# A list scheduler given measured durations and new ranks, and the last output tile cut in the middle

## The chip, the cores and the metric

The kernel runs on one core of a Trainium2 chip, in one launch. The metric is the device time of that launch in microseconds, as the median of several runs. TensorE (PE) multiplies matrices, VectorE (DVE) and ScalarE (ACT) work on tiles in SBUF and PSUM, GpSimd (POOL) on tiles in SBUF alone, and SyncE (SP) issues the transfers.

## The reference

One transformer block on 512 tokens of width 1024, in float32. In short:

```python
h = rmsnorm(x, attn_pre_g)
q_n, kc, vc, ksl, vsl, kwn, vwn, g_n, q_s, k_s, v_s = split(h @ w_in)
# 8 heads: compressed + selected + windowed attention, gated; 8 heads: 128-wide window with sinks
o_nsa = gate0 * attend(q_n, compress(kc), compress(vc)) + gate1 * attend(q_n, ksl, vsl) + gate2 * attend(q_n, kwn, vwn)
o_swa = window_attend(q_s, k_s, v_s, sinks)
x = x + rmsnorm(concat(o_nsa, o_swa) @ w_o, attn_post_g)
a, u = split(rmsnorm(x, mlp_pre_g) @ w_gate_up)            # 2 x 2816
y = (gelu(causal_conv3(a)) * u) @ w_down
x = x + rmsnorm(y, mlp_post_g)
out = x + (p @ w_ple) * sigmoid(x @ w_ple_gate)
```

## The kernel before, in words

Every large product is made of three matmuls on values split in a high part and a low part (`hi*hi + lo*hi + hi*lo`). So each operand, weights, probabilities and activations alike, costs a rounding copy (the high part, on ScalarE) and a subtraction (the low part, on VectorE or GpSimd) before TensorE can use it.

The stages: loading and the value projections; compression of keys and values; the first query projections; then the *planned part*: attention, the other projections, the output projection, its norm, the per-layer embedding and the first products of the MLP; then the MLP with its own written order, and the last gate.

The planned part is emitted by class `Plan`. Each operation is added with a name (a tuple), an engine, a duration in us, a rank, the operations it comes after, and the buffers that it takes and uses. `Plan.order` is a list scheduler: it keeps a clock for each engine and again and again picks the operation that can start first by the given durations; among those that are ready when their engine is free, the lowest rank goes first. The operations are emitted in that order and each engine executes its own in that order. The durations thus never reach the chip, only the order does.

Attention is cut in 16 units, `ORDER`: a kind (nsa or swa), a group of 4 heads and a tile of 128 queries. A unit's ranks are its number less one for scores and softmax, its number for the products. Operations are known by their first letter(s) and the length of the name, which is how `SHIFT` re-ranks a kind:

- `s`: scores on TensorE into one of three banks `ps` (L598, L599). `m`: on VectorE the biased minimum of such a bank, called a *soft* here (L602; 4 fields for nsa, 3 for swa), which frees the bank. `e`: the exponential on ScalarE (L606). `rc`: reciprocals on VectorE (L714, L724). `px`, `pe`, `pr`: the same for the compressed branch, on POOL, ScalarE and VectorE. `gc`, `pm`: the gate column of the compressed branch and its multiplication, on POOL. `g`: scaling of a head's probabilities on POOL (L594).
- `t`: transposes of the probabilities on TensorE into one of two banks `pt` (L807, for the compressed block L800). `h` and `l`: high part on ScalarE (L811) and low part on VectorE (L815) of such a bank, for the compressed block in four pieces of 32 rows (`l` with 4 fields, L834). The last of them frees the bank. `v`: the products with the values (L822, L839). `up`, `ad`, `oh`, `ol`: the sum of the two halves of the result, and its high and low parts.
- `f`: steps of the projections (L258 to L262) and `op`: steps of the output projection (L1001 to L1003), three matmuls each. They rank behind everything of the units and are called *fill*: TensorE takes them when nothing of the units can start. Their weights need `w` (a load on SP), `wh` (ScalarE) and `wl` (POOL, L915); the output projection's need `ow`, `oh` (3 fields) and `ol`. `hi` are high parts of later weights.

The last stage, `ple_gate`, makes 8 output tiles. The last one is cut in two runs of columns, so that its end is short:

```python
pieces = [(0, T)] if c < KC - 1 else [(0, LASTCUT), (LASTCUT, T)]
for n, (a, b) in enumerate(pieces):
    ...
    self.gemm(ps[:, a:b], wt, [x[:, :, a:b] for x in self.x2])
    ...
    nc.scalar.activation(s, ps[:, a:b], AF.Sigmoid)
    nc.vector.tensor_mul(s, s, self.e[c // 2][:, c % 2, a:b])
    ...
    nc.sync.dma_start(io["out"][c * P : (c + 1) * P, a:b], o)
```

Of the kernel before, what the change touches and what calls it, by code (L numbers as in the profile page):

```python
# [49 lines left out]
YTAG = ["kn"] * 3 + ["tt"] + ["p"] * 2 + ["pt"] * 2 + ["u"] * 14  # L50


LASTCUT = 352
FORMS = (-5.6, 5.5)
NPLAIN = 5
SEVEN = range(8, NFF)
# [13 lines left out]
PAIRS = 2  # L70
THIRD = (NCMP + 2 * T) // 3
UNITS = 3
SHIFT = {("l", 4): 0.88, ("pe2", 2): -4.0, ("v", 4): 1.95, ("oe", 3): -1.52, ("e", 3): 1.52, ("s", 4): -0.33,
         ("pm", 2): 1.91, ("pn", 2): -0.47, ("g", 4): 1.14, ("oh", 2): 0.97, ("fe", 3): 0.12, ("rc", 3): -1.18,
         ("gc", 2): 1.04, ("m", 4): 0.11, ("n", 4): -2.1}
ORDER = [(k, g, qt) for k in "ns" for g in range(2) for qt in (3, 0, 2, 1)]
PLE_PS = ["mm", "s", "mm", "s", "mm", "s", "o", "s"]
ETAG = ["pt", "u", "u", "u"]
# [4 lines left out]
class Plan:  # L83
# [15 lines left out]

    def add(self, name, eng, us, rank, f, after=(), take=(), use=(), land=0.0, beside=None):  # L100
        assert name not in self.ops, name
        if rank < 100:
            rank += SHIFT.get((name[0], len(name)), 0.0)
        self.ops[name] = (eng, us, rank, f, [a for a in after if a], list(take), land, beside)
        for _, token in take:
            self.users.setdefault(token, set()).add(name)
        for token in use:
            self.users.setdefault(token, set()).add(name)
# [74 lines left out]
class Block:  # L183
# [1244 lines left out]
    def up_rest(self, pending):  # L1428
# [37 lines left out]
        def sums(j, n):  # L1466
            m0, m1 = w[j]["m"]
            if n == 0:
                w[j]["s13"] = self.u([P, D], F32, "pt")
                keep(add(w[j]["s13"][:, :W], m1[:, :W], m1[:, W:]))  # L1470
            s13 = w[j]["s13"]
            if n == 1:
                w[j]["s24"] = self.u([P, D], F32, "tt")
                keep(sub(w[j]["s24"][:, :W], s13[:, :W], m0[:, :W]))
            if n == 2:
                keep(sub(w[j]["s24"][:, W:], m0[:, W:], w[j]["s24"][:, :W]))  # L1476
            if n == 3:
                keep(sub(s13[:, W:], m0[:, :W], m1[:, :W]))
# [29 lines left out]
        def evict(j, n):  # L1508
            z = st[j]
            a = self.am[j % 2]  # L1510
            if n == 0:
                z["s"] = self.sp.tile([P, H], F32, tag="s1", name=self.nm("s1"), bufs=2)
                keep(act.activation(z["s"], z["p"][0], AF.Copy))
                z["e"] = self.s([P, 2, H], tag="as")
            if n in (1, 3):
                keep(act.activation(z["e"][:, n // 2, :], z["p"][0], AF.Copy))
            if n == 2:
                keep(add(a[:, 2 : 2 + H], z["s"], z["p"][1]))
            if n == 4:
                keep(add(z["e"][:, 1, :], z["e"][:, 1, :], z["p"][2]))  # L1520
            if n == 6:
                keep(add(a[:, 2 + H :], z["e"][:, 0, :], z["p"][2]))  # L1522
# [434 lines left out]
    def ple_gate(self):  # L1957
# [3 lines left out]
        for c in range(KC):  # L1961
            if c < NB:
                ps = self.pss[c]
            else:
                wt = ahead.get(c) or self.weight(io["wpg"][c])
            pieces = [(0, T)] if c < KC - 1 else [(0, LASTCUT), (LASTCUT, T)]
            for n, (a, b) in enumerate(pieces):
# [85 lines left out]
```

## Time and profile before

| | |
|---|---|
| median of 3 runs | 643.38 us (643.23 to 643.42) |
| the profiled execution's own time | 642.44 us |
| its span, first to last instruction | 640.7 us |
| TensorE busy | 633.0 us |
| VectorE, ScalarE, GpSimd busy | 532.1, 385.3, 128.1 us |
| planned attention in the trace | about 80 to 205 us |
| granted TensorE clock, mean | 0.999 |

A row of the timeline has the start and the duration in us, the engine, the line, the operation, out<-in by the program's names without their numbers, the shape and a count. An idle time of the engine before it stands in brackets with what ended it. Consecutive matmuls overlap in their records: the next starts before the record of the last has ended. A row of stretches has, for each engine, the busy time and the number of instructions.

### The profile page before, as it was taken

To read this page: it belongs to the slowest core of one execution; us is meant where nothing else is said; L and a number is where in the kernel's file an instruction comes from. 1 tells how busy PE (TensorE), PEld (TensorE's weight loads), DVE (VectorE), ACT (ScalarE), POOL (GpSimd) and SP (SyncE) were. 2 spreads that over 40 slices of the span, in tenths; PEclk is the share of its full clock that TensorE was granted. 3 is DMA by queue.
4 is the path that set the end of the run, shared out by engine and by line. 5 is a ranking of instruction groups with operands and counts; after the bars stand their busy time and mean duration, and the time that the engine had idled before them with its cause. 6 is when DMAs were issued, how large, how long until landed. Compare 5 with 4: busy or idle time off the path is not lost.

```text
span 640.7 us, 10962 instructions
## 1 busy us (share of the span) xinstructions
PE 633.0 (99%) x3925; PEld 567.6 (89%) x3925; DVE 532.1 (83%) x1133; ACT 385.3 (60%) x746; POOL 128.1 (20%) x213
## 2 busy tenths in 40 slices
PE   8999999999999999999999999999999999999997
PEld 8988888788887888888889999999998899999986
DVE  7794778989897559799999999999978887796972
ACT  7453689889999456265565656556656444362351
POOL 1120398667585320111000000000000000000000
PEclk9999999999999999999999999999999999999999
DMA  8437632210216456322223324233222233485031
GB/s 306 144 125 236 166 94 75 58 50 27 74 61 220 153 196 252 123 69 97 99 100 132 110 89 132 71 128 127 63 68 65 80 103 120 120 321 221 1 132 67
DMA packets 27864, 78.07 MB, mean 122 GB/s; under 512 B 3489, under 2 KB 5025, under 8 KB 27809
## 3 DMA queue, kind: packets, MB, share of 16 engines
q1 hardware_dynamic: 27664, 77.28, 36.2%
q8 instruction: 31, 0.51, 0.3%
q14 instruction: 25, 0.20, 0.1%
q10 hardware_dynamic: 144, 0.08, 0.1%
HBM read 63.72 MB, written 6.29 MB: 109 GB/s over the span
## 4 chain that ended last, share of the span: by engine, by line
PE 91%; DVE 4%; ACT 3%; issue 1%; DMA 1%; ACTq 0%; DVEq 0%
PE strassen_pss L1505 3%; PE strassen_pss L1502 3%; PE strassen_pss L1506 3%; PE nsa_pst L807 2%; PE nsa_pso L822 2%; PE strassen_psmm L1502 2%; PE strassen_psmm L1505 2%; PE strassen_psmm L1506 2%; PE strassen_pst L1502 2%; PE strassen_pst L1505 2%; PE strassen_pst L1506 2%; PE r_pss L1189 2%; PE r_psmm L1189 2%; PE nsa_pss L598 1%; PE fill_psmm L261 1%; PE fill_psmm L262 1%
## 5 line engine op out<-in xcount | busy, mean ns | idle before, releaser
L594 POOL TENSOR_SCALAR nsa_u<-nsa_u,nsa_nrc,gate 128x512 f32<-128x512 f32 (+3 forms) x64 | 38.7, 617 | 43.5 <-PE nsa_pss L599 30.1
L1828 POOL TENSOR_TENSOR mlpdown_s<-mlpdown_s,mlpdown_s 128x512 f32<-128x512 f32 x1 | 1.3, 1297 | 197.3 <-ACT mlpdown_s L1826 197.3
L1464 DVE TENSOR_TENSOR strassen_u<-strassen_u,strassen_u 128x1024 fp32r<-128x1024 f32 x31 | 37.7, 1218 | 0.2 <-ACT strassen_u L1460 0.2
L606 ACT ACTIVATE nsa_u<-nsa_u,nsa_nnm 128x512 f32<-128x512 f32 (+3 forms) x64 | 35.3, 553 | 3.1 <-DVE nsa_nnm L602 2.8
L815 DVE TENSOR_TENSOR nsa_u<-nsa_pst,nsa_u 128x512 fp32r<-128x512 f32 x40 | 27.0, 688 | 9.8 <-ACT nsa_u L811 9.6
L1460 ACT ACTIVATE strassen_u<-strassen_u 128x1024 fp32r<-128x1024 f32 x31 | 32.4, 1049 | 0.4 <-DVE strassen_u L1476 0.4
L1538 DVE SCALAR_TENSOR_TENSOR strassen_s<-mlpup_u,cols,strassen_s 128x512 f32<-128x512 f32 x36 | 26.9, 748 | 1.5 <-ACT strassen_s L1536 0.9
L822 PE MATMUL nsa_pso<-nsa_u,vnatural_u 128*128 128x512 f32 x80 | 28.0, 422 | 0.0
L811 ACT ACTIVATE nsa_u<-nsa_pst 128x512 fp32r<-128x512 f32 x40 | 23.3, 594 | 4.7 <-PE nsa_pst L807 4.0
L602 DVE CUSTOM_DVE_ANT_0 nsa_u<-nsa_pss,biastables_u 128x320 f32<-128x320 f32 (+3 forms) x64 | 24.7, 413 | 1.0 <-PE nsa_pss L599 0.9
L807 PEld LDWEIGHTS nsa_pst<-ident,nsa_u 128*128 128x128 f32 x160 | 18.9, 140 | 6.9 <-issue 1.3
L1738 ACT ACTIVATE mlpdown_u<-mlpdown_u 128x1024 fp32r<-128x1024 f32 (+1 forms) x15 | 15.1, 1011 | 15.6 <-DVE mlpdown_u L1757 15.3
L807 PE MATMUL nsa_pst<-ident,nsa_u 128*128 128x128 f32 x160 | 23.5, 274 | 0.7 <-DVE nsa_u L815 0.5
L1742 DVE TENSOR_TENSOR mlpdown_u<-mlpdown_wr,mlpdown_u 128x640 fp32r<-128x640 f32 (+1 forms) x19 | 17.5, 919 | 7.0 <-ACT mlpdown_u L1738 4.1
L1738 ACT ACTIVATE mlpdown_u<-mlpdown_wr 128x640 fp32r<-128x640 f32 (+1 forms) x19 | 15.0, 788 | 13.8 <-DMA mlpdown_wr<-in_dn_dram 3.1
L1505 PE MATMUL strassen_pss<-strassen_u,strassen_u 128*128 128x256 f32 x80 | 22.5, 282 | 0.0
L1502 PE MATMUL strassen_pss<-strassen_u,strassen_u 128*128 128x256 f32 x80 | 22.5, 281 | 0.0
L1742 DVE TENSOR_TENSOR mlpdown_u<-mlpdown_u,mlpdown_u 128x1024 fp32r<-128x1024 f32 (+1 forms) x15 | 17.5, 1170 | 5.9 <-ACT mlpdown_u L1738 5.7
L1506 PE MATMUL strassen_pss<-strassen_u,strassen_u 128*128 128x256 f32 x80 | 22.4, 280 | 0.0
L1541 ACT ACTIVATE strassen_s<-strassen_s 128x512 f32<-128x512 f32 x18 | 11.4, 632 | 17.1 <-DVE strassen_s L1538 17.1
L1536 ACT ACTIVATE strassen_s<-mlpup_u,cols 128x512 f32<-128x512 f32 x18 | 14.7, 815 | 10.5 <-DVE mlpup_u L1522 10.4
L1464 DVE TENSOR_TENSOR strassen_u<-strassen_wr,strassen_u 128x1024 fp32r<-128x1024 f32 x17 | 20.7, 1218 | 0.3 <-ACT strassen_u L1460 0.3
(690 smaller groups left out, 2582.7 us busy)
## 6 DMA issues: line engine op xcount, KB each, us to landing
strassen_wr<-in_gu_dram SPq DMA_DIRECT2D x17, 512.0 KB, 4.2
strassen_u<-in_gu_dram SPq DMA_DIRECT2D x17, 512.0 KB, 3.3
mlpdown_wr<-in_dn_dram SPq DMA_DIRECT2D x9, 512.0 KB, 3.5
mlpdown_wr<-in_dnx_dram SPq DMA_DIRECT2D x10, 320.0 KB, 2.9
r_wr<-in_gu_dram SPq DMA_DIRECT2D x6, 512.0 KB, 3.2
projq_wr<-in_win_dram SPq DMA_DIRECT2D x5, 512.0 KB, 3.3
loadx_u<-in_xT_dram SPq DMA_DIRECT2D x8, 256.0 KB, 4.7
compress_u<-projk_u SPq DMA_DIRECT2D x16, 128.0 KB, 2.3
```

The costliest lines, as they stand in the source:

```text
L594: self.tc.keep_in_program_order(self.nc.gpsimd.tensor_scalar(ap, ap, col, gate, op0=ALU.mult, op1=ALU.mult))
L606: self.tc.keep_in_program_order(self.nc.scalar.activation(p, p, AF.Exp, bias=nm, scale=-1.0, accum_out=sm))
L807: keep(nc.tensor.transpose(pt[:, r * P : (r + 1) * P], src, self.ident))
L815: keep(nc.vector.tensor_sub(t[:, 1, :], u["pt", j], t[:, 0, :].bitcast(F32)))
L822: keep(nc.tensor.matmul(u["po"], v, u["t", j][:, part, :], start=start, stop=u["left"] == 0))
L1460: keep(act.activation(hi, src, AF.Copy))
L1464: keep(sub(lo, src, hi.bitcast(F32)))
L1502: r = mm(ps, hi[:, o], x[:, 0, :], start=fresh and p == 0, stop=False, skip_group_check=not fresh)
L1505: mm(ps, lo[:, o], x[:, 0, :], start=False, stop=False, skip_group_check=not fresh)
L1506: mm(ps, hi[:, o], x[:, 1, :], start=False, stop=p == Q - 1, skip_group_check=not fresh)
L1738: keep(act.activation(z[key, 0], z[key][:, :n], AF.Copy))
L1742: keep(eng.tensor_sub(z[key, 1], z[key][:, :n], z[key, 0].bitcast(F32)))
```

## The change

Three edits. `SHIFT` gets four new values and six new kinds: swa exps 0.3 sooner, the gated compressed probabilities (`pm`) 0.9 sooner, their gate column (`gc`) 1.1 later, nsa softs (`m`, 4 fields) 0.3 later; newly low parts of projection weights (`wl`) 1.3 sooner, low parts of probabilities (`l`, 3 fields) 1.2 sooner, high parts of output-projection weights 1.3 later, swa softs (`m`, 3 fields) 1.1 later, high parts of later weights 0.3 later, transposes 0.6 later. A table `TAKES` replaces durations in the planner, by kind, name length and the old value; TensorE's, but for transposes, are also raised by 1%. `LASTCUT` goes from 352 to 256.

```diff
-LASTCUT = 352
+LASTCUT = 256
 ...
-         ("pm", 2): 1.91, ("pn", 2): -0.47, ("g", 4): 1.14, ("oh", 2): 0.97, ("fe", 3): 0.12, ("rc", 3): -1.18,
-         ("gc", 2): 1.04, ("m", 4): 0.11, ("n", 4): -2.1}
+         ("pm", 2): 1.01, ("pn", 2): -0.47, ("g", 4): 1.14, ("oh", 2): 0.97, ("fe", 3): 0.12, ("rc", 3): -1.18,
+         ("gc", 2): 2.14, ("m", 4): 0.41, ("n", 4): -2.1, ("wl", 2): -1.3, ("l", 3): -1.2, ("oh", 3): 1.3,
+         ("m", 3): 1.1, ("hi", 2): 0.3, ("t", 3): 0.6}
 ...
+         ("pe", 2, 0.2): 0.201, ("oh", 2, 0.31): 0.308, ("oe", 3, 0.48): 0.494, ("l", 4, 0.21): 0.3,
+         ("rc", 3, 0.08): 0.178, ("rc", 3, 0.14): 0.26, ("pr", 2, 0.2): 0.38, ("ad", 3, 0.42): 0.431,
 ...
     def add(self, name, eng, us, rank, f, after=(), take=(), use=(), land=0.0, beside=None):
         assert name not in self.ops, name
+        us = TAKES.get((name[0], len(name), round(us, 2)), us)
+        if eng == "PE" and (name[0], len(name)) != ("t", 3):
+            us *= 1.01
         if rank < 100:
             rank += SHIFT.get((name[0], len(name)), 0.0)
```

From the tables on, lines of the changed kernel are numbered 10 higher. Three places show what the new order does. On TensorE, at the end of the last nsa unit and the start of the swa units (171 us in the trace of before): `nsa_pso` are products, `swa_pst` transposes, `swa_pss` scores, `fill_psmm` a step of the output projection. Before:

```order
L822 MATMUL nsa_pso_2256<-nsa_u_2276,vnatural_u_334 128x512
L807 MATMUL swa_pst_2306<-ident,swa_u_2135 128x128 x4
L822 MATMUL nsa_pso_2256<-nsa_u_2276,vnatural_u_334 128x512
L598 MATMUL swa_pss_2297<-projq_u_812,nsa_u_1791 128x256
L599 MATMUL swa_pss_2297<-projq_u_813,nsa_u_1791 128x256
L807 MATMUL swa_pst_2320<-ident,swa_u_2135 128x128 x4
L839 MATMUL nsa_pso_2256<-compressout_u_725,vc 128x256 x2
```

and now:

```order
L832 MATMUL nsa_pso_2253<-nsa_u_2268,vnatural_u_334 128x512 x2
L608 MATMUL swa_pss_2289<-projq_u_812,fill_u_1782 128x256
L609 MATMUL swa_pss_2289<-projq_u_813,fill_u_1782 128x256
L1011 MATMUL fill_psmm_2304<-nsa_u_1301,nsa_u_2112 128x512
L1012 MATMUL fill_psmm_2304<-nsa_u_1302,nsa_u_2112 128x512
L1013 MATMUL fill_psmm_2304<-nsa_u_1301,nsa_u_2113 128x512
L817 MATMUL swa_pst_2312<-ident,swa_u_2136 128x128 x4
L817 MATMUL swa_pst_2321<-ident,swa_u_2136 128x128 x4
L849 MATMUL nsa_pso_2253<-compressout_u_725,vc 128x256 x2
```

Both groups of transposes moved behind the scores and behind a step of fill; the two products, of the high and of the low part, stand together.

On VectorE, where units 0 to 3 meet (97 us in the trace of before): `compressout_u` are the four low pieces of unit 0's compressed block, `nsa_pss` the score banks that softs read. Before:

```order
L815 TENSOR_TENSOR nsa_u_1192<-nsa_pst_1176,nsa_u_1192 128x512
L834 TENSOR_TENSOR compressout_u_725<-nsa_pst_1169,compressout_u_725 32x128 x2
L714 RECIPROCAL nsa_nrc_985<-nsa_nsm_984 128x2
L834 TENSOR_TENSOR compressout_u_725<-nsa_pst_1169,compressout_u_725 32x128 x2
L602 ISA nsa_pc_986,nsa_nnm_983<-nsa_pss_1195,biastables_u_457 128x32
L602 ISA nsa_nnm_983 128x1
L602 ISA nsa_u_1194,nsa_nnm_983<-nsa_pss_1195,biastables_u_457 128x384
```

and now:

```order
L844 TENSOR_TENSOR compressout_u_725<-nsa_pst_1167,compressout_u_725 32x128 x4
L825 TENSOR_TENSOR nsa_u_1192<-nsa_pst_1174,nsa_u_1192 128x512
L612 ISA nsa_pc_979,nsa_nnm_976<-nsa_pss_1159,biastables_u_457 128x32
L612 ISA nsa_nnm_976 128x1
L612 ISA nsa_u_1158,nsa_nnm_976<-nsa_pss_1159,biastables_u_457 128x384
L612 ISA nsa_nnm_976 128x1
L724 RECIPROCAL nsa_nrc_978<-nsa_nsm_977 128x2
```

The low pieces stand together, with the reciprocal no longer between them, and they and the low part of unit 1 have moved ahead of one more head's softs (bank 1159; in the old order that head's softs came before all of these rows).

On GpSimd, at the second weight of the fill (85 us in the trace of before): `128x1024` is a weight's low part (`wl`), the `128x128` scalings are those of unit 1. Before:

```order
L737 TENSOR_TENSOR nsa_gc_1036<-nsa_nrc_828,gate 128x4
L594 TENSOR_SCALAR nsa_u_941<-nsa_u_941,nsa_nrc_939,gate 128x128 x6
L936 TENSOR_TENSOR fill_u_1065<-fill_s_973,fill_u_1065 128x512
L915 TENSOR_TENSOR nsa_u_1071<-fill_wr_846,nsa_u_1070 128x1024
L594 TENSOR_SCALAR nsa_u_941<-nsa_u_941,nsa_nrc_939,gate 128x128 x2
```

and now:

```order
L925 TENSOR_TENSOR fill_u_1000<-fill_wr_846,fill_u_999 128x1024
L727 TENSOR_TENSOR nsa_pc_942<-nsa_pc_942,nsa_nnm_939 128x128
L604 TENSOR_SCALAR nsa_u_910<-nsa_u_910,nsa_nrc_828,gate 128x512
L604 TENSOR_SCALAR nsa_u_943<-nsa_u_943,nsa_nrc_941,gate 128x128
L946 TENSOR_TENSOR fill_u_1064<-fill_s_1002,fill_u_1064 128x512
L604 TENSOR_SCALAR nsa_u_943<-nsa_u_943,nsa_nrc_941,gate 128x128 x7
```

The weight's low part stands ahead of all eight scalings of unit 1, where it stood behind six of them, and the gate column has moved further back.

More of the change, by code (lines that the diff above doesn't have):

```diff
@@ L72 @@
 UNITS = 3
-SHIFT = {("l", 4): 0.88, ("pe2", 2): -4.0, ("v", 4): 1.95, ("oe", 3): -1.52, ("e", 3): 1.52, ("s", 4): -0.33,
-         ("pm", 2): 1.91, ("pn", 2): -0.47, ("g", 4): 1.14, ("oh", 2): 0.97, ("fe", 3): 0.12, ("rc", 3): -1.18,
-         ("gc", 2): 1.04, ("m", 4): 0.11, ("n", 4): -2.1}
+SHIFT = {("l", 4): 0.88, ("pe2", 2): -4.0, ("v", 4): 1.95, ("oe", 3): -1.52, ("e", 3): 1.22, ("s", 4): -0.33,
[3 rows of a table added]
+TAKES = {("h", 3, 0.47): 0.496, ("h", 4, 0.26): 0.282, ("up", 2, 0.5): 0.51, ("nh", 2, 0.53): 0.62,
[5 rows of a table added]
 ORDER = [(k, g, qt) for k in "ns" for g in range(2) for qt in (3, 0, 2, 1)]
```

3 rows, old and new, of the table TAKES are left out of this document.

## The prediction

> **What bounds the kernel now.** I read the page's first part, then the busy time of each engine in stretches, then TensorE's waits, and last the timeline at each wait.
>
> ```profile
> span 640.7 us, 10962 instructions
> PE 633.0 (99%) x3925; PEld 567.6 (89%) x3925; DVE 532.1 (83%) x1133; ACT 385.3 (60%) x746; POOL 128.1 (20%) x213
> core 0: us, PE busy (x) PEld busy (x) DVE busy (x) ACT busy (x) POOL busy (x), PEclk, DMA share, GB/s
> 80.00:100.00 20.00, 19.68 (x114) 16.68 (x113) 15.46 (x64) 17.46 (x52) 18.98 (x28) 1.00 0.37 111
> 100.00:120.00 20.00, 19.60 (x114) 16.18 (x112) 17.52 (x74) 17.05 (x50) 14.48 (x23) 1.00 0.28 70
> 120.00:140.00 20.00, 19.87 (x112) 16.16 (x112) 17.60 (x79) 17.51 (x52) 15.82 (x28) 1.00 0.16 43
> 140.00:160.00 20.00, 19.59 (x116) 16.57 (x114) 17.61 (x73) 18.09 (x53) 12.60 (x23) 1.00 0.07 21
> 160.00:180.00 20.00, 19.44 (x121) 16.20 (x119) 17.70 (x62) 18.75 (x59) 11.17 (x23) 1.00 0.23 61
> 180.00:205.00 25.00, 24.81 (x142) 20.79 (x141) 20.84 (x60) 24.52 (x65) 19.75 (x34) 1.00 0.45 157
> 205.00:245.00 40.00, 40.00 (x183) 32.81 (x182) 25.15 (x36) 22.84 (x37) 9.98 (x10) 1.00 0.54 185
> ```
>
> TensorE sets the time: 633.0 of 640.7 us. Its clock is full (1.00) in these rows. The edits act in the planned part (in the trace, the attention from about 80 us on) and in the last output tile. In the attention (80 to 205 us) TensorE's idle time is 0.32 + 0.40 + 0.13 + 0.41 + 0.56 + 0.19 = 2.01 us, and from 205 to 245 it is nil, so the out-projection and the norm have nothing to give.
>
> Idle time is not the whole of a wait, because a matmul's record outlasts the start of the next one:
>
> ```profile
> 81.64 0.40 PE L261 MATMUL fill_psmm<-loadx_u,projq_wh 128*128 128x512 f32 x1
> 81.88 0.39 PE L262 MATMUL fill_psmm<-loadx_u,projq_wh 128*128 128x512 f32 x1
> 82.23 0.41 PE L598 MATMUL nsa_pss<-compress_u,projq_u 128*128 128x384 f32 x1
> 98.88 0.28 PE L800 MATMUL nsa_pst<-ident,nsa_pc 128*128 128x128 f32 x1
> 99.47 0.36 PE L598 MATMUL nsa_pss<-compress_u,projq_u 128*128 128x256 f32 x1 [0.32 <-DVE nsa_nnm L602]
> ...
> 171.60 0.28 PE L599 MATMUL swa_pss<-projq_u,nsa_u 128*128 128x256 f32 x1
> 172.32 0.63 PE L807 MATMUL swa_pst<-ident,swa_u 128*128 128x128 f32 x4 [0.44 <-DVE compressout_u L834]
> ...
> 201.94 0.48 PE L822 MATMUL swa_pso<-swa_u,vnatural_u 128*128 128x512 f32 x1
> 202.50 0.66 PE L807 MATMUL swa_pst<-ident,swa_u 128*128 128x128 f32 x4
> ```
>
> A 512-column matmul starts 0.23 us after the one before it, though its record is 0.39 long. A wait is therefore start to start less that spacing: 0.12 us at 81.88 (the first), 0.34 at 201.94 (the last). Counted so, with each form's own undisturbed spacing, the timeline from 80 to 205 us has 13 waits above 0.12 us, 4.18 us together, 0.32 each in the mean. That fits the idle time: 2.01 us plus 13 times the hidden 0.16 us is 4.1. VectorE ended every one of them:
>
> - **Low parts and small operations**, 7 waits, 2.52 us: five by the low part of a probability tile (L815), 0.42, 0.20, 0.39, 0.23, 0.34; one by L834 (the low parts of a compressed block), 0.60 at 171.6; one by the reciprocal L714, 0.35.
> - **Softs** (L602, the biased minimum that frees a score bank) and one output sum, 6 waits, 1.66 us.
>
> Why VectorE was late is seen ahead of the wait at 98.88:
>
> ```profile
> 97.22 0.58 DVE L834 TENSOR_TENSOR compressout_u<-nsa_pst,compressout_u 32x128 fp32r<-32x128 f32 x2
> 97.83 0.17 DVE L714 RECIPROCAL nsa_nrc<-nsa_nsm 128x2 f32<-128x2 f32 x1
> 98.03 0.59 DVE L834 TENSOR_TENSOR compressout_u<-nsa_pst,compressout_u 32x128 fp32r<-32x128 f32 x2
> ```
>
> The planner of before counts 0.21 us for an L834 piece and 0.08 for this reciprocal; they take 0.29 and 0.17. Over the five instructions that is 0.41 us of VectorE time that the plan did not know of, near the 0.49 that TensorE then waited.
>
> **The change part by part.** No arithmetic is added or taken away in the attention.
>
> *The durations (TAKES) and the 1% on TensorE's.* They have no price on the chip; they alter the order alone. What they should do is let the planner place a projection or out-projection step (three 512-column matmuls, 3 x 0.23 = 0.68 us) where VectorE is late. At 171.6 the order shows exactly this: three `fill` matmuls now stand ahead of the transposes that waited 0.60 us. 0.68 covers it, the wait goes. In the last swa units a fill step also comes between the transposes and the products that stood alternately around 201.94: 0.34 goes. The total of fill is unchanged, so a step used here is missing later; the stretch from 205 us, where no wait is left, is where that would show.
>
> *Low parts of probabilities sooner (1.2 units of rank), softs later (+0.30 and +1.10).* A low is L815, 0.69 us; a soft is about 0.48 (99.25 less 98.77, below). A low that no longer stands behind a soft frees its transpose bank about 0.48 us sooner, more than each of the other four L815 waits (0.20 to 0.42): these go. The reciprocal's 0.35 has no row that excludes either end (0 to 0.35); I take it as gone, since its duration is now right to 0.01 (0.178 given, 0.17 seen). Sum gone: 2.52.
>
> ```profile
> 98.77 0.55 DVE L602 CUSTOM_DVE_ANT_0 nsa_u<-nsa_pss,biastables_u 128x384 f32<-128x384 f32 x1
> 99.25 0.55 DVE L602 CUSTOM_DVE_ANT_0 nsa_u<-nsa_pss,biastables_u 128x384 f32<-128x384 f32 x1
> ```
>
> What is late next is the softs: a low ahead of them holds their score bank 0.69 us longer. I leave the 1.66 us of their waits as they are and add one new wait of mean size, 0.32. Bounds: all 13 waits go, -4.18; none goes, 0. Balance taken: -2.52 + 0.32 = -2.20.
>
> *Weights' low parts sooner, the gate column later, on POOL.* Costed at nothing: no wait of the 13 was ended by POOL. The cover is POOL's lead; without it the price is one L915, 2.39 us (rivals). *Other ranks (high parts of weights, exps, swa transposes) and SP's queue,* whose loads are re-ordered with them: 0, since no wait was ended by ScalarE or a DMA; bounds are one mean wait either way, 0.32.
>
> *The last tile in 256 + 256 columns instead of 352 + 160.*
>
> ```profile
> 605.73 0.28 PE L258 MATMUL norm_pss<-norm_u,mlpdown_u 128*128 128x256 f32 x1
> 609.57 0.28 PE L262 MATMUL norm_psmm<-norm_u,mlpdown_u 128*128 128x256 f32 x1
> 630.36 0.32 PE L258 MATMUL plegate_psmm<-norm_u,plegate_wh 128*128 128x352 f32 x1
> 634.22 0.24 PE L258 MATMUL plegate_pss<-norm_u,plegate_wh 128*128 128x160 f32 x1
> 634.42 0.46 ACT L1974 ACTIVATE plegate_s<-plegate_psmm 128x352 f32<-128x352 f32 x1 [3.27 <-PE plegate_psmm L262]
> 634.92 0.53 DVE L1975 TENSOR_TENSOR plegate_s<-plegate_s,mlpdown_u 128x352 f32<-128x352 f32 x1 [2.31 <-ACT plegate_s L1974]
> 636.53 0.27 PE L258 MATMUL plegate_pss<-norm_u,plegate_wh 128*128 128x160 f32 x1
> 637.07 0.30 ACT L1974 ACTIVATE plegate_s<-plegate_pss 128x160 f32<-128x160 f32 x1 [2.18 <-PE plegate_pss L262]
> 637.40 0.32 DVE L1975 TENSOR_TENSOR plegate_s<-plegate_s,mlpdown_u 128x160 f32<-128x160 f32 x1 [1.40 <-ACT plegate_s L1974]
> out_dram<-plegate_s SPq DMA_DIRECT2D x1, 176.0 KB, 1.8
> out_dram<-plegate_s SPq DMA_DIRECT2D x1, 80.0 KB, 1.6
> ```
>
> 24 matmuls of 352 columns take 634.22 - 630.36 = 3.86 us. Of the 160-column ones, 21 take 636.53 - 634.22 = 2.31, 0.110 each, 24 take 2.64. The same count of 256 columns: 32 in 609.57 - 605.73 = 3.84, 0.120 each, 48 take 5.76. TensorE gains 3.86 + 2.64 - 5.76 = 0.74 us, on the path. Behind it the last piece is 96 columns wider: ScalarE by (0.46 - 0.30)/192 per column, +0.08; two VectorE operations by (0.53 - 0.32)/192, +0.21; the store, half the way from 1.6 to 1.8, +0.10. Net -0.35. The first piece's chain starts at about 633.4 and is long done when the second piece ends.
>
> The row of 160 columns is odd: 0.110 us, hardly under the 0.120 of 256. The Trainium skill ("TensorE: Matmul & The Clock Gate", Back-to-back issue gap) gives a warm matmul's spacing as columns/2.4 ns plus 2.5 ns. By that rule alone both splits cost an estimated 24 x (149 + 69) = 48 x 109 = 5.2 us, the edit gains nothing on TensorE and the sum for the tail is +0.39. The same page (LDWEIGHTS) gives an estimated 107 ns for loading 128 columns of weights, under which no matmul of a new weight tile can stay; this trace's 0.110 agrees with the second rule, not with the first alone.
>
> **Sum.** -2.20 - 0.35 = -2.55 us against the profiled execution, whose span is 640.7 and whose own time is 642.44 us. That one is 0.94 us under the median of the runs, 643.38 (643.23 to 643.42); carried to the median: 640.8 us.
>
> **Rivals.**
> - *The waits only change places.* ScalarE is busy 18.75 of 20 and 24.52 of 25 us in the stretches from 160 to 205: what TensorE saves there must still pass ScalarE, and the lows put first delay the softs as much as they help the transposes. Against it: 2.53 us of the waits lie before 160, where ScalarE idles 2 to 3 us in each 20. Then only the tail counts: 643.0 us.
> - *POOL becomes the releaser* (the other side). From 80 to 100 us POOL is busy 18.98 of 20 us, and in the new order a weight's low part stands ahead of all eight scalings of unit 1, which fed transposes without a wait so far, where it stood behind six.
>
> ```profile
> 87.28 1.31 POOL L936 TENSOR_TENSOR fill_u<-fill_s,fill_u 128x512 fp32r<-128x512 f32 x1
> 88.54 2.39 POOL L915 TENSOR_TENSOR nsa_u<-fill_wr,nsa_u 128x1024 fp32r<-128x1024 f32 x1
> ```
>
>   If nothing covers the 2.39 us and VectorE's waits stay, 643.38 - 0.35 + 2.39 = 645.4 us. It decides for slower once over 1.64 us of it are uncovered, that is, when not even two fill steps (1.36) stand in. Against it: the weight that comes sooner is what lets fill steps start sooner.
> - *The tail gains nothing*, the matmul's time going with its columns alone: 640.8 + 0.74 = 641.5 us. The 0.110 us row speaks against it.
>
> **How the numbers follow.** 0.2% is 1.29 us, about what a measurement of this kernel tells from no change. The forecast has 0.59 (own range 639.2 to 642.0), the tail rival 0.04: faster 0.63. Waits that change places: 0.27, same. POOL: 0.10, slower. The range reaches from all 13 waits gone with the tail (643.38 - 4.18 - 0.35 = 638.9, rounded up) to the second case plus three new waits of mean size (643.0 + 0.96, about 643.9); it leaves out POOL's case and little else.
>
> **What would show it.** TensorE's idle time from 80 to 205 us near 1 us instead of 2.01; no wait ended by L834, and those ended by the low parts of probabilities (L825 by the new numbering) gone or under 0.1; the waits that are left ended by softs. In the tail, 48 matmuls of 256 columns in 5.8 us, and 0.35 us less from 630.36 to the end. I am wrong if TensorE's waits name POOL's scalings, if new waits appear from 205 us on because fill ran out, or if the idle time stays at 2 us under other names.

## The result and the profile after

| | before | after |
|---|---|---|
| median of the runs | 643.0 us (642.45 to 643.42, 6 runs) | 639.35 us (639.23 to 640.36, 6 runs) |
| profiled execution: own time, span | 642.44, 640.7 us | 639.23, 637.5 us |
| TensorE busy | 633.0 us | 631.3 us |
| first score to first matmul of the MLP | 203.17 us | 200.66 us |
| first matmul of the last output tile to the end | 10.37 us | 9.99 us |

The changed kernel takes 0.9947 of the time (95% interval 0.9934 to 0.996). The forecast was 640.8. The first lines of the page after, and its stretches with the columns of before:

```profile
span 637.5 us, 10954 instructions
PE 631.3 (99%) x3925; PEld 567.6 (89%) x3925; DVE 531.5 (83%) x1133; ACT 383.3 (60%) x746; POOL 128.7 (20%) x213
core 0: us, PE busy (x) PEld busy (x) DVE busy (x) ACT busy (x) POOL busy (x), PEclk, DMA share, GB/s
80.00:100.00 20.00, 20.00 (x117) 17.32 (x115) 15.16 (x63) 16.28 (x46) 19.19 (x29) 1.00 0.35 106
100.00:120.00 20.00, 20.00 (x116) 16.82 (x115) 18.07 (x78) 18.20 (x54) 14.72 (x24) 1.00 0.30 75
120.00:140.00 20.00, 19.89 (x116) 16.89 (x115) 17.66 (x77) 17.04 (x51) 15.74 (x28) 1.00 0.16 40
140.00:160.00 20.00, 19.90 (x119) 16.99 (x118) 18.66 (x75) 18.27 (x55) 13.44 (x23) 1.00 0.08 21
160.00:180.00 20.00, 19.60 (x122) 16.58 (x121) 18.00 (x68) 18.91 (x60) 11.96 (x27) 1.00 0.23 61
180.00:205.00 25.00, 25.00 (x137) 20.65 (x136) 20.87 (x56) 24.59 (x64) 18.84 (x32) 1.00 0.52 178
205.00:245.00 40.00, 40.00 (x183) 33.08 (x182) 26.08 (x38) 23.75 (x39) 10.04 (x10) 1.00 0.55 186
```

TensorE's idle time from 80 to 205 us is 0.11 + 0.10 + 0.40 = 0.61 us, where it was 2.01. Counted from start to start, as in the prediction, eight waits above 0.12 us are left, 1.93 us together, where 13 had 4.18. The excess of all matmuls over the usual spacing of their shape, small waits included, fell from 4.6 to 2.6 us between 80 and 160 us; from 160 to 220 only from 2.4 to 2.1. The largest wait that is left:

```profile
171.56 0.40 PE L1013 MATMUL fill_psmm<-nsa_u,nsa_u 128*128 128x512 f32 x1
...
172.15 0.28 PE L609 MATMUL swa_pss<-projq_u,nsa_u 128*128 128x256 f32 x1
172.79 0.63 PE L817 MATMUL swa_pst<-ident,swa_u 128*128 128x128 f32 x4 [0.37 <-DVE swa_u L825]
```

What VectorE did meanwhile:

```profile
170.24 0.48 DVE L612 CUSTOM_DVE_ANT_0 swa_u<-swa_pss,biastables_u,nsink 128x256 f32<-128x256 f32 x1
...
171.53 0.48 DVE L612 CUSTOM_DVE_ANT_0 swa_u<-swa_pss,biastables_u,nsink 128x256 f32<-128x256 f32 x1
171.93 0.08 DVE L612 DVE_READ_ACCUMULATOR2_ANT swa_nm<- 128x1 f32 x1
171.95 1.29 DVE L825 TENSOR_TENSOR swa_u<-swa_pst,swa_u 128x512 fp32r<-128x512 f32 x2
```

The fill step of which the prediction spoke starts at 169.29, and the transposes behind it, at 169.99, no longer wait; but the group behind the next fill step, shown above, does, 0.53 us start to start, because its low part (the first of the two in the last row) stands behind four softs. In the tail, first matmul of each run and the last one, then the work behind it:

```profile
627.53 0.28 PE L268 MATMUL plegate_psmm<-norm_u,plegate_wh 128*128 128x256 f32 x1
630.40 0.28 PE L268 MATMUL plegate_pss<-norm_u,plegate_wh 128*128 128x256 f32 x1
633.16 0.28 PE L272 MATMUL plegate_pss<-norm_u,plegate_wh 128*128 128x256 f32 x1
633.48 0.38 ACT L1984 ACTIVATE plegate_s<-plegate_pss 128x256 f32<-128x256 f32 x1 [2.49 <-PE plegate_pss L272]
633.89 0.42 DVE L1985 TENSOR_TENSOR plegate_s<-plegate_s,mlpdown_u 128x256 f32<-128x256 f32 x1 [1.99 <-ACT plegate_s L1984]
634.35 0.42 DVE L1987 TENSOR_TENSOR plegate_s<-plegate_s,mlpdown_u 128x256 f32<-128x256 f32 x1
out_dram<-plegate_s SPq DMA_DIRECT2D x2, 128.0 KB, 1.7
```

The 3.2 us between the two spans are 2.5 in the planned part, 0.4 in the tail and 0.3 in the stages between them, from the MLP to the norm, whose instructions and order are the same. That last piece is spread: over all 14 profiles of this study the stages from the MLP to the norm take 340.7 to 341.5 us, and the stages ahead of the attention end at 69.65 to 70.55. So in the experiments the planned part is measured by itself, from the first score to the first matmul of the MLP, in one profile of each kernel. How far one profile of it can be trusted is seen from orders that were profiled twice: the old one took 203.17 and 203.62 us (the second, with the tail alone, holds 0.3 us of a late load, see the last section), the new one 200.66 and 200.75 (the second with another cut). Its two ends in the kernel before and after:

```profile
69.79 0.32 PE L598 MATMUL nsa_pss<-compress_u,projq_u 128*128 128x352 f32 x1
272.96 0.39 PE L258 MATMUL mlpup_pso<-r_u,r_u 128*128 128x512 f32 x1
69.74 0.32 PE L608 MATMUL nsa_pss<-compress_u,projq_u 128*128 128x352 f32 x1
270.40 0.40 PE L268 MATMUL mlpup_pso<-r_u,r_u 128*128 128x512 f32 x1
```

### The profile page after: what moved, and what is told of

Its sections match the earlier page's. It is cut to its first block, busy times and chain, and to the rows that moved or that the text cites. A ratio compares the mean times of both kernels' runs of the same rounds, so it can differ in the third digit from the quotient of the medians.

```text
span 637.5 us, 10954 instructions
## 1 busy us (share of the span) xinstructions
PE 631.3 (99%) x3925; PEld 567.6 (89%) x3925; DVE 531.5 (83%) x1133; ACT 383.3 (60%) x746; POOL 128.7 (20%) x213
## 4 chain that ended last, share of the span: by engine, by line
PE 94%; ACT 4%; DVE 1%; issue 1%; ACTq 0%
PE strassen_pss L1515 3%; PE strassen_pss L1512 3%; PE strassen_pss L1516 3%; PE strassen_psmm L1515 2%; PE nsa_pst L817 2%; PE strassen_psmm L1516 2%; PE strassen_psmm L1512 2%; PE nsa_pso L832 2%; PE strassen_pst L1515 2%; PE strassen_pst L1512 2%; PE strassen_pst L1516 2%; PE r_pss L1199 2%; PE r_psmm L1199 2%; ACT nsa_u L616 1%; PE fill_psmm L272 1%; PE fill_psmm L271 1%
## 5 line engine op out<-in xcount | busy, mean ns | idle before, releaser
L825 DVE TENSOR_TENSOR nsa_u<-nsa_pst,nsa_u 128x512 fp32r<-128x512 f32 x40 | 26.9, 686 | 6.7 <-ACT nsa_u L821 6.1
L821 ACT ACTIVATE nsa_u<-nsa_pst 128x512 fp32r<-128x512 f32 x40 | 23.1, 594 | 4.2 <-PE nsa_pst L817 3.9
```

The lines of the kernel that those rows point to most:

```text
L825: keep(nc.vector.tensor_sub(t[:, 1, :], u["pt", j], t[:, 0, :].bitcast(F32)))
```

## Experiments: the parts of the change

Four kernels, each the kernel before with a part of the change.

**The tail alone.**

```diff
-LASTCUT = 352
+LASTCUT = 256
```

> The kernel before with one edit: the last output tile in two runs of 256 columns (LASTCUT 256) instead of 352 and 160. The plan of the attention is the old one. Theory: the tail is worth what the two profiles differ by there, 10.37 to 9.99 us from the first matmul of the last tile to the end, so 0.4 us (0.06%) less, about 642.6 where the kernel before has 643.0; in its trace the 48 matmuls start 0.120 us apart. Rival (a matmul's pace follows its columns alone, so 48 x 256 streams as long as 24 x 352 + 24 x 160): the 0.74 us of TensorE are not gained and the later work costs its 0.39, so 643.4. The times can hardly tell these two apart; the rows of the last tile can.

642.61 us, ratio 0.9993 (0.9984 to 1.0002): not to be told from no change, as expected. Its last tile goes from 631.51 to the end at 641.49, 9.98 us, as in the changed kernel. In the rows the tail's 0.4 us are there without the rest of the change.

**Durations alone, ranks alone, both without the tail.**

```diff
+TAKES = {...}
+        us = TAKES.get((name[0], len(name), round(us, 2)), us)
+        if eng == "PE" and (name[0], len(name)) != ("t", 3):
+            us *= 1.01
```

> The kernel before with the table TAKES and TensorE's 1% alone: old SHIFT, old cut of 352. Theory A (the planner lacked VectorE's true durations; given them, it puts fill where VectorE is late, whatever the ranks): most of the planned part's 2.35 us is here, 640.7 to 641.3 where the kernel before has 643.0, and TensorE's waits above 0.12 us between 80 and 205 us fall from 4.18 us to about 2. Rival B (the ranks do it, low parts ahead of softs): within 0.5 us of the kernel before. Rival C (durations and ranks only work together, each was tuned for the other): the time is that of before or above it, up to 645, with other waits than before's.

```diff
-SHIFT = {... ("e", 3): 1.52, ... ("pm", 2): 1.91, ... ("gc", 2): 1.04, ("m", 4): 0.11, ("n", 4): -2.1}
+SHIFT = {... ("e", 3): 1.22, ... ("pm", 2): 1.01, ... ("gc", 2): 2.14, ("m", 4): 0.41, ("n", 4): -2.1,
+         ("wl", 2): -1.3, ("l", 3): -1.2, ("oh", 3): 1.3, ("m", 3): 1.1, ("hi", 2): 0.3, ("t", 3): 0.6}
```

> The kernel before with the new SHIFT alone: old durations, old cut of 352. Theory A (durations): within 0.7 us of the kernel before, 642.3 to 643.7. Rival B (ranks): low parts ahead of softs by themselves take the waits that VectorE's low parts ended, so about 640.7 and waits of about 2 us. Rival C (only together): 643 or above.

> The changed kernel with the old cut of 352 in the last tile: durations and ranks together. All theories say what the marks of the two profiles say up to the last tile: 2.3 to 2.8 us less than before, 640.2 to 640.7, and 0.4 above the changed kernel. If it came out at 639.4, the tail would be worth nothing; its rows must then show the last tile from first matmul to the end at 10.0 instead of 10.4 us.

Durations alone: 642.84 us, ratio 1.0001 (0.9991 to 1.001). Ranks alone: 648.76, 1.0082 (1.0069 to 1.0095). Both: 640.87, 0.9968 (0.9956 to 0.9981), just above the 640.2 to 640.7 that was expected, with a planned part of 201.92 us in a profile that holds 0.9 us of the late load (last section). Neither half gains anything, one of them loses 5 us, and together they gain: rival C. Theories A and B fall, and with B what the prediction put down to the ranks by themselves. The durations alone help in one place and cost in another. The largest waits of that kernel in the planned part, summed (engine, line, waited for, us in total, times, longest):

```profile
PE nsa_pso L831 <- ACT swa_u L615: 0.8, 1, 0.8
PE swa_pso L831 <- ACT swa_u L820: 0.6, 1, 0.6
PE nsa_pst L816 <- DVE nsa_u L824: 0.5, 1, 0.5
PE swa_pst L816 <- DVE compressout_u L843: 0.4, 1, 0.4
```

and two of its stretches:

```profile
120.00:140.00 20.00, 20.00 (x115) 17.08 (x114) 17.67 (x78) 18.16 (x53) 17.22 (x30) 1.00 0.18 47
160.00:180.00 20.00, 17.75 (x114) 14.66 (x113) 17.34 (x60) 17.32 (x55) 9.15 (x23) 1.00 0.13 31
```

Ahead of 160 us the excess falls from 4.6 to 3.0 us. From 160 to 180, where the last nsa units meet the first swa units, TensorE idles 2.25 us. The profile names ScalarE for the two largest waits, but a name there is only the engine whose signal came last, and an nsa product doesn't use swa's exponentials (L615). It needs the one bank `po`, which the output sums of the unit before (L881) free, and the rows of these sums reach up to it:

```profile
167.07 0.59 ACT L874 ACTIVATE nsa_s<-nsa_pso 64x512 f32<-64x512 f32 x1
167.76 0.85 DVE L881 TENSOR_TENSOR nsa_s<-nsa_pso,nsa_s 64x256 f32<-64x256 f32 x2 [0.17 <-ACT nsa_s L874]
168.76 0.93 PE L831 MATMUL nsa_pso<-nsa_u,vnatural_u 128*128 128x512 f32 x3 [0.78 <-ACT swa_u L615]
```

The sums on VectorE end at 168.61, and they waited for ScalarE's copy (L874), which had stood behind exponentials. At the second wait (176.54) the sums end at 176.39 and the high part (L820) at 176.48. The plan tells the idle time itself: with the new durations and the old ranks, the planner's own clock has 4.5 us of gaps on TensorE, nearly all from the 84th to the 107th us of the plan. With the ranks alone, the largest new wait is at the row statistics:

```profile
PE r_pss L1190 <- ACT r_u L1167: 2.3, 1, 2.3
```

Its plan, made with the old durations, has a gap of 2.47 us ahead of that step too.

## Experiments: is the planner's clock right?

That gave a new theory, H: with the measured durations the planner's clock is nearly that of the chip, so ranks can be chosen by it; with the old ones it wasn't. The next four kernels are the changed kernel with other ranks, forecast from the planner's clock.

**The rank of the nsa softs at 0.11 and at 0.31.**

```diff
-         ("gc", 2): 2.14, ("m", 4): 0.41, ("n", 4): -2.1, ...
+         ("gc", 2): 2.14, ("m", 4): 0.11, ("n", 4): -2.1, ...
```

> The changed kernel with one number put back: nsa softs at 0.11 as before instead of 0.41. Theory H (with the measured durations the planner's own clock is about right, so a gap of TensorE that it plans is there on the chip): the planner now leaves TensorE 3.7 us of gaps instead of 0.4, nearly all of them between the 80th and the 106th us of the plan (about 165 to 190 us of the trace, five of them in front of transposes), so 3.3 us more than the changed kernel: 642.6 or, against the kernel before, a ratio of 0.9995. Rival R (ten re-ranks share the gain, each is worth some tenths): 639.4 to 639.9, ratio below 0.996. Rival D (durations do it alone and ranks are noise): like the changed kernel, 0.9947.

```diff
-         ("gc", 2): 2.14, ("m", 4): 0.41, ("n", 4): -2.1, ...
+         ("gc", 2): 2.14, ("m", 4): 0.31, ("n", 4): -2.1, ...
```

> The changed kernel with the same number at 0.31, which is nearer to the new value of 0.41 than the old one is. Theory H (the planner's clock is right): it plans 7.8 us of gaps, 7.4 more than in the changed kernel, from the 82nd us of the plan on, so about 646.7, a ratio of 1.006: worse than with the old value, though the step is a third of it. Rival R (each re-rank is worth a few tenths, in proportion to its step): within 0.2 us of the changed kernel, 0.9947 to 0.995.

Softs at 0.11: 643.11 us, ratio 1.0001 (0.9993 to 1.001): one number takes the whole gain back. Softs at 0.31: 648.87, 1.0083 (1.0069 to 1.0097), worse than at 0.11 and at 0.41. Both lose, as H has it (642.6 and 646.7), the second 2 us more than it says; R and D fall. The loss is not in proportion to the step, and does not even grow with it. The scheduler only compares ranks, so a small step can turn the order of two operations around or do nothing. In the second kernel waits follow one another where gaps were planned, here from 171 to 174 us:

```profile
171.00 0.66 PE L817 MATMUL nsa_pst<-ident,nsa_u 128*128 128x128 f32 x4 [0.17 <-DVE nsa_u L825]
172.55 0.66 PE L817 MATMUL nsa_pst<-ident,nsa_u 128*128 128x128 f32 x4 [0.89 <-DVE nsa_u L825]
173.72 0.30 PE L810 MATMUL nsa_pst<-ident,nsa_pc 128*128 128x128 f32 x1 [0.51 <-DVE nsa_u L825]
```

Ahead of the longest of them VectorE does softs of a swa unit, whose products come later, and only then the low part that TensorE waits for:

```profile
170.86 0.48 DVE L612 CUSTOM_DVE_ANT_0 swa_u<-swa_pss,biastables_u,nsink 128x256 f32<-128x256 f32 x1
...
171.53 0.35 DVE L612 CUSTOM_DVE_ANT_0 swa_u<-swa_pss,biastables_u,nsink 128x128 f32<-128x128 f32 x1
171.81 0.08 DVE L612 DVE_READ_ACCUMULATOR2_ANT swa_nm<- 128x1 f32 x1
171.81 0.69 DVE L825 TENSOR_TENSOR nsa_u<-nsa_pst,nsa_u 128x512 fp32r<-128x512 f32 x1
```

**GpSimd's four re-ranks put back.**

```diff
-SHIFT = {... ("pm", 2): 1.01, ... ("gc", 2): 2.14, ... ("wl", 2): -1.3, ... ("hi", 2): 0.3, ...}
+SHIFT = {... ("pm", 2): 1.91, ... ("gc", 2): 1.04, ...}
```

> The changed kernel with the four re-ranks put back that move almost nothing but GpSimd's work: low parts of weights, gate column, gated compressed probabilities, high parts of later weights. 47 places of GpSimd's order change, 4 of TensorE's. Theory (GpSimd is idle for a quarter and more of every stretch and ends none of the waits above 0.12 us): the changed kernel's time, ratio 0.994 to 0.9955, and no wait of TensorE ended by GpSimd. Rival (the weight's low part ahead of the scalings of unit 1 lets the fill start sooner, and part of the gain before 100 us hangs on it): 0.5 to 1 us above, 0.9955 to 0.9965, with the waits before 100 us back. The prediction's own rival (the low part's place makes GpSimd late) would make this kernel faster than the changed one, by up to the 4.6 us priced there.

640.34 us, 0.9956 (0.9943 to 0.9969); the planned part takes 200.76 us against 200.66, with the same eight waits (1.96 us), none of them ended by GpSimd. These four did nothing, for or against. (The expectation's premise is too wide: from 80 to 100 us the changed kernel's GpSimd is busy 19.19 of 20 us. It still ends no wait there.)

**All ranks searched anew.**

```diff
-SHIFT = {("l", 4): 0.88, ("pe2", 2): -4.0, ("v", 4): 1.95, ... ("l", 3): -1.2, ... ("m", 3): 1.1, ...}
+SHIFT = {("l", 4): 0.88, ("pe2", 2): -6.4, ("v", 4): -0.05, ... ("l", 3): -4.0, ... ("m", 3): 4.1, ...}
```

> The changed kernel with other ranks for nearly all kinds, found by trying ranks on the planner's own clock with the new durations, also raised by 2% on VectorE and ScalarE: it plans 0.05 us of gaps where the changed kernel has 0.41. Theory H (the planner's clock is about right): 0.3 us less than the changed kernel, 639.0, ratio 0.994. Rival (what is left, 1.9 us of waits, comes from what the planner doesn't know, so one good plan is like another or worse by chance): 639.4 to 640.5, ratio 0.9947 to 0.996, with waits of 1.5 to 3 us at other places.

641.7 us, 0.9982 (0.9972 to 0.9992): the planner saw 0.36 us less than in the changed kernel, the chip had 1.3 more in the planned part and 11 waits, 3.2 us. Here H misses, and the rival's 640.5 is passed too. The planner's clock tells plans apart that differ by some microseconds, not by tenths.

## Experiments: is it VectorE's time?

The entries of TAKES add 7.8 us in all to what the planner counts for VectorE. Nearly all of it is four entries: the reciprocals, 24 x 0.098 = 2.35 and 8 x 0.12 = 0.96; the sum of the compressed block, 8 x 0.18 = 1.44; its low parts, 32 x 0.09 = 2.88; together 7.6 us (the 6.7 of the expectations below leaves out the 0.96). Theory V: the old order was good for the durations it was given, and TensorE waited because VectorE ran later. Then the old order must gain if VectorE gets the time back, and the new one lose if VectorE gets more work.

**The order before, VectorE relieved.**

```diff
-keep(nc.vector.tensor_sub(place(r, True, t), u["pt", j][32 * r : 32 * r + 32, :P],
-                          place(r, False, t).bitcast(F32)))
+keep(nc.vector.tensor_sub(place(r, True, t)[:, :16], u["pt", j][32 * r : 32 * r + 32, :16],
+                          place(r, False, t)[:, :16].bitcast(F32)))
```

> The kernel before, its order untouched, with VectorE's low parts of the compressed block on 16 of their 128 columns (the other columns of the low part are left out). The 32 operations took 0.29 us each in the trace; if they come out at 0.13 to 0.19 us, VectorE is relieved of 3 to 5 us, most of the 6.7 us by which the old planner had its reciprocals (24 x 0.098 and 8 x 0.12 us), sums (8 x 0.18) and these low parts (32 x 0.09) too short. Theory V (the old order is good for the durations it was given; TensorE waited because VectorE ran later than the planner thought): with VectorE back at the planned pace the waits fall from 4.2 us to 1 to 2, and the time by 2 to 3.5 us, to 639.5 to 641, a ratio of 0.9945 to 0.997. Rival (the old order itself is worse, for instance by where fill stands, or ScalarE sets the pace): within 0.6 us of before, ratio above 0.999.

640.13 us, ratio 0.9952 (0.9939 to 0.9964). Its page has these stretches, and the shortened operations:

```profile
100.00:120.00 20.00, 19.99 (x121) 17.07 (x120) 17.59 (x78) 17.87 (x52) 15.13 (x24) 1.00 0.32 79
140.00:160.00 20.00, 20.00 (x121) 17.09 (x120) 17.72 (x76) 18.61 (x56) 14.45 (x26) 1.00 0.08 22
160.00:180.00 20.00, 19.94 (x125) 16.87 (x125) 17.59 (x66) 19.40 (x60) 11.47 (x24) 1.00 0.23 60
L834 DVE TENSOR_TENSOR compressout_u<-nsa_pst,compressout_u 32x16 fp32r<-32x16 f32 x32 | 5.5, 171 | 0.9 <-ACT compressout_u L830 0.3
```

With 32 x (0.287 - 0.171) = 3.7 us taken off VectorE, not one instruction of the order moved, TensorE's waits fall from 4.18 to 1.38 us and the planned part from 203.17 to 200.17. That TensorE waited in the old order because of VectorE's time is shown. The row of 160 to 180 us settles a rival too: ScalarE is busy 19.40 of 20 us there and TensorE 19.94, so in the kernel before, at 18.75, ScalarE did not set the pace.

Another rival is that such a relief helps any order. It was not tried on the changed kernel. On the planner's clock with the new durations (computed, not measured) the old order's 4.7 us of gaps fall to 1.5 with this relief, and to 0.5 with the four entries at their old values; the new order's fall only from 0.4 to 0.3.

**The new order, VectorE loaded.**

```diff
-lambda r=r, u=u: keep(nc.vector.reciprocal(u["rc"][:, r, 1:3], u["sm"][:, r, 1:3])),
+lambda r=r, u=u: [keep(nc.vector.reciprocal(u["rc"][:, r, 1:3], u["sm"][:, r, 1:3])) for _ in range(2)],
```

> The changed kernel, its order untouched, with the 24 small reciprocals of a head done twice: VectorE has 24 x 0.16 = 3.8 us more work in the nsa units than its planner knows, about the 6.7 us by which the old planner was off, halved. Theory V (waits come from VectorE running later than planned): TensorE's waits rise from 1.9 to 4.5 to 5 us and the time by 2 to 3, to 642 to 643, a ratio of 0.998 to 1.0. Rival (VectorE, busy for 16 to 18 of 20 us, has the slack to take 0.5 us more in a unit): within 0.6 us of the changed kernel, 0.994 to 0.996.

641.61 us, ratio 0.9982 (0.9973 to 0.999), at the near end of what V expected; of these 2.3 us the planned part has 1.65 (202.31), and the rest lies where the kernels are the same. So the added work costs, though in the planned part less than the 2 to 3 us expected, and the waits above 0.12 us rise only to 2.23, not to 4.5: the rest is spread over smaller ones (the whole excess from 80 to 220 us rises from 4.6 to 6.2). VectorE's slack takes more than half of the added work.

**The four durations taken out again.**

```diff
-         ("pe", 2, 0.2): 0.201, ("oh", 2, 0.31): 0.308, ("oe", 3, 0.48): 0.494, ("l", 4, 0.21): 0.3,
-         ("rc", 3, 0.08): 0.178, ("rc", 3, 0.14): 0.26, ("pr", 2, 0.2): 0.38, ("ad", 3, 0.42): 0.431,
+         ("pe", 2, 0.2): 0.201, ("oh", 2, 0.31): 0.308, ("oe", 3, 0.48): 0.494, ("ad", 3, 0.42): 0.431,
```

> The changed kernel with four entries of TAKES taken out: both reciprocals, the sum of the compressed block and its low parts are planned at their old durations (0.08, 0.14, 0.2, 0.21 us), the other nineteen and the ranks are the new ones. The planner sees little harm: 0.9 us of gaps instead of 0.4, a plan 0.4 us longer. Theory V (these four are the durations that mattered, and a plan made without them is late on the chip): an order made so, put against the new durations, has 5.5 us of gaps, so 4 to 5 us more than the changed kernel, 643.5 to 644.5, ratio 1.0 to 1.003, with many waits of 0.15 to 0.4 us behind VectorE before 160 us. Rival (what the planner sees is what counts, or the ranks carry the gain): 0.4 us above the changed kernel, ratio 0.995 to 0.9965.

643.68 us, ratio 1.0015 (1.0006 to 1.0024). A plan that looks 0.4 us longer to its planner is 4.1 us longer on the chip (204.74), the chip taking the side of the measured durations; the waits above 0.12 us are 14, 4.5 us, again. The table puts the kernels together: each order's end on the planner's clock with the new durations (computed, each engine doing its operations in the order given), and the planned part in the trace, both less the changed kernel's.

| order | computed, us | measured, us |
|---|---|---|
| before | +4.3 | +2.5 |
| durations alone | +4.1 | +2.8 |
| ranks alone | +7.2 | +7.3 |
| softs at 0.11 | +3.3 | +4.2 |
| softs at 0.31 | +7.4 | +9.2 |
| GpSimd's ranks old | 0 | +0.1 |
| ranks searched | -0.4 | +1.3 |
| four durations old | +5.1 | +4.1 |

The profiles of softs at 0.11 and 0.31 hold 0.6 and 1.0 us of the late load. The clock sees which plans are some microseconds worse; for the kernel before and the durations alone it overstates by more than one.

**Another cut.**

```diff
-LASTCUT = 256
+LASTCUT = 320
```

> The changed kernel with the last tile in runs of 320 and 192 columns, between the old cut (352 and 160) and the new one (256 and 256). Theory (each of these matmuls has a new weight tile, and its pace does not fall below 0.11 us): 24 x 0.146 + 24 x 0.11 = 6.1 us of TensorE instead of 5.76, and 0.1 us less in the work behind the shorter second run, so the stretch from the first matmul of the last tile to the end is 10.2 us, between 9.99 and 10.37. Rival (pace by columns: 24 x 512 columns take the same time however they are cut): the stretch is 9.9 us or less, since only the work behind gets shorter. The run's time can't tell 0.2 us; the rows can. It also stands for the changed kernel on this chip: 0.2 us above it.

640.03 us, 0.9953 (0.994 to 0.9966), 0.4 to 0.7 us above the changed kernel where 0.2 was expected, which the run's time can't tell. The last tile to the end takes 10.14 us, and the rows agree with a floor of the pace:

```profile
628.20 0.30 PE L268 MATMUL plegate_psmm<-norm_u,plegate_wh 128*128 128x320 f32 x1
631.71 0.25 PE L268 MATMUL plegate_pss<-norm_u,plegate_wh 128*128 128x192 f32 x1
634.26 0.28 PE L272 MATMUL plegate_pss<-norm_u,plegate_wh 128*128 128x192 f32 x1
```

The 192-column matmuls start (634.26 - 631.71)/23 = 0.111 us apart, no faster than the 0.110 of 160 columns. So 256 and 256, of which neither run reaches the floor, is the best of the three cuts. No experiment beat the changed kernel.

## Why the prediction came out

- *What bounds it* held: waits behind VectorE in the attention, none after 205 us, 40.00 of 40 busy there in both.
- *The sum* held: -2.51 in the planned part for a forecast of -2.20. *Which* waits go did not. Two of the prediction's names were wrong first: the name in brackets is only the signal that came last before the start. Its wait "by the reciprocal" (0.35 at 146.57) is one for a score bank, which a soft frees; the reciprocal, no input of a score, stands beside it in the rows below. And of the six put down to softs and a sum, one (0.27 at 118.43) is a transpose whose low part ended at 118.28. So before had 2.45 us of waits for low parts and 1.73 for softs and a sum. The softs and the sum, which were to stay, keep 0.31 (0.15 and 0.16). The low parts, of which nothing was to stay, keep 1.15 (L825 0.26 and 0.53, L844 0.17 and 0.19). New are two ended by ScalarE's high parts (L821), 0.28 and 0.19, for the one of 0.32 expected: -1.42 - 1.30 + 0.47 = -2.25. So the signs that the prediction named, no wait left behind a low part and only softs among the rest, failed. At 171.6 the fill step covered its wait, and the next one arose behind four softs. The wait at 201.94 went.
- *The step that failed* is "low parts of probabilities sooner, softs later". It took four waits behind L815, 0.42 + 0.20 + 0.39 + 0.23 = 1.24 us, to end because a low part would no longer stand behind a soft. In the rows a soft stands directly ahead of it for two of them only (0.42 and 0.39); the 0.20 comes after VectorE itself waited for a high part of ScalarE, the 0.23 after two output sums (both below). And the ranks by themselves are worth nothing: alone they lose 5 us. What the runs show in its place is that the gain is the agreement of order and durations. The size came out partly by luck: both ways of counting draw on the same pool of 4.18 us, of which a good plan leaves some two.
- *Why VectorE was late* was read rightly from the rows at 97 us (0.41 us too little planned over five instructions), and the experiments bear it out. The prediction used it for the two fill steps and the 0.35 alone, 1.29 of its 2.52 us. It was not followed to its end, that such a plan is wrong everywhere at once.
- *Waits that only change places* (ScalarE as the pace from 160 us): little was gained there, 0.3 us of excess, but the relieved kernel shows TensorE at 19.94 of 20 beside a ScalarE at 19.40. The place is right and ScalarE's pace as the reason is not.
- *GpSimd at nothing* held; the rival of a late weight fell with its four ranks put back. Of the *other ranks at nothing*, the high parts of later weights were put back with GpSimd's and did nothing; the exps, the transposes and the high parts of the output projection's weights were not tried by themselves. A bound of one mean wait, 0.32 us, is too tight for a rank: the step of the softs from 0.41 to 0.31 cost some 8 us.
- *The tail*: -0.38 for -0.35. TensorE -0.76 (6.39 to 5.63 us, first start to last; forecast 0.74), ScalarE 0.38 for 0.30, VectorE 0.42 for 0.32 twice, the store 1.7 for 1.6. The rival fell: its pace goes with the columns alone, and the pace here stops falling at 0.110 to 0.111 us. It went by the Trainium skill's columns/2.4 + 2.5 ns ("TensorE: Matmul & The Clock Gate", Back-to-back issue gap), which the Trainium skill gives for an isolated matmul: an estimated 82.5 ns for 192 columns; the trace has 111. The Trainium skill's weight load of an estimated 107 ns (same page, LDWEIGHTS) is near that. That no matmul of a new weight tile can go below its load is the prediction's inference, which that page of the Trainium skill does not state; it fits the last tile's streams (160 and 192 columns) but not every row: in the attention a product with another weight tile starts 0.03 us after a transpose (170.78 after 170.75).
- The median fell below the forecast by 1.45 us. 0.3 of that is the planned part and 0.3 the stages between. The other 0.8 is the step from a profile to the median: 0.94 us were added, as in the kernel before, and the changed kernel's profile lies only 0.12 below its median. Such offsets differ from kernel to kernel: nearly the same order gave 640.34 with GpSimd's ranks put back.

The rows for the waits at 112.67, 146.57 and 168.10, in the kernel before:

```profile
111.92 0.69 DVE L815 TENSOR_TENSOR nsa_u<-nsa_pst,nsa_u 128x512 fp32r<-128x512 f32 x1 [0.56 <-ACT nsa_u L811]
...
146.35 0.08 DVE L602 DVE_READ_ACCUMULATOR2_ANT nsa_nnm<- 128x1 f32 x1
146.35 0.16 DVE L714 RECIPROCAL nsa_nrc<-nsa_nsm 128x2 f32<-128x2 f32 x1
146.57 0.36 PE L598 MATMUL nsa_pss<-compress_u,projq_u 128*128 128x256 f32 x1 [0.18 <-DVE nsa_nrc L714]
...
166.48 0.85 DVE L872 TENSOR_TENSOR nsa_s<-nsa_pso,nsa_s 64x256 f32<-64x256 f32 x2
167.36 1.29 DVE L815 TENSOR_TENSOR nsa_u<-nsa_pst,nsa_u 128x512 fp32r<-128x512 f32 x2
```

## What to carry to other kernels

When a planner orders the work, compare its durations with the trace before anything else, those of many small operations first: here 0.09 to 0.18 us missing in each of 72 cost 4.1 us in the planned part, more than the 2.5 that the change brings there. Change durations and ranks together, and judge neither half alone: here each half gave nothing or a loss. A list scheduler's rank is a switch, not a dial. Its own clock, once right, tells plans apart that differ by microseconds; for the last few tenths only the chip does. And ask of each name in a wait whether the waiting operation uses what that engine made.

## What was not expected of the hardware

A small VectorE operation is nearly all fixed cost: from 128 to 16 columns the low part fell from 0.287 to 0.171 us, 1.04 ns a column, which leaves an estimated 0.15 us at no columns at all. The reciprocal of two columns takes 0.16. The Trainium skill ("VectorE: DVE Perf Modes", The TRN2 errata) has a table with 120 cycles and one for each column from PSUM at 0.96 GHz, an estimated 0.14 us for 16 columns; the trace's slope agrees and its record is 0.03 longer. The same section of the Trainium skill has (columns + 151)/0.96 ns for an fp32 add from SBUF to SBUF, an estimated 0.174 and 0.291 us for 16 and 128 columns, and the trace is within 0.004 of both.

One load ahead of the attention sometimes comes late. Four of the fourteen profiles (the tail alone, durations and ranks without the tail, softs at 0.11 and at 0.31) wait 0.3, 0.9, 0.6 and 1.0 us for the compressed keys (a DMA) at the first scores; the other ten don't, with the same program up to there. In those four the eight copies are issued later, the first 3.2 to 4.0 us ahead of the first score; in the other ten it is 4.4 to 4.6. Each takes some 2.3 us as before. Why they are issued later was not tried.
